# Storing each output tile as two halves from two queues, SyncE and GpSimd, in a mixture-of-experts dispatch kernel

## The chip, the cores and the metric

The kernel runs on one core of one Trainium2 chip. The metric is the device time of one execution in microseconds: before the change the median of three runs is 240.65 us (240.26 to 240.80). The profiled execution took 240.13 us, of which the trace covers a span of 238.3 us, from the first instruction to the last.

## The reference

Every token's row of 512 fp32 values is written out twice (k = 2), each copy multiplied by one of the token's two expert weights. The expert indices are an input, but they don't enter the result.

```python
batch, seq, hidden, n_experts = 16, 1024, 512, 8      # k = 2

def reference(x, expert_indices, expert_weights):
    x_expanded = x[:, :, np.newaxis, :].repeat(k, axis=2)
    weights = expert_weights[..., np.newaxis]
    return (x_expanded * weights).astype(np.float32)
```

The input x is 16384 rows of 2 KB, 33.55 MB; the output is twice that, 67.11 MB; the weights are 0.13 MB. There is one multiplication for each output element and nothing else.

## The kernel before

The 16384 tokens are cut into eight tiles of 2048 tokens. Partition p of a tile holds 16 consecutive tokens, so that what one partition loads is 32 KB contiguous in x and what it stores is 64 KB contiguous in the output. The list `groups` (line 35) and the function `rows` (line 48) say this.

Three pools hold the buffers. `w_tile` has all weights, 256 for each partition, loaded at the start by eight small transfers on SyncE's queue (line 57). `x_tile` has two buffers of 32 KB per partition. `o_tile` has two buffers; one is shaped `[P, 2, HALF * row + PAD]` (line 88), two halves of eight tokens each, 32 KB per partition and half. The padding of eight elements keeps the two halves apart in the buffer.

`load(i)` (lines 71 to 79) loads a whole x tile, 4 MB (4096 KB in the profile), with one transfer on ScalarE's queue (line 78). Tiles 0 and 1 are loaded ahead. The main loop (line 83) then does, for tile i and each of its 16 tokens t, two multiplications of 128 x 512 elements by a weight for each partition: the first copy on VectorE (`tensor_scalar`, line 99), the second on ScalarE (`mul`, line 93). Both write to half `h = t // HALF` of `o_tile`.

The stores are all on SyncE's queue (line 109). Tile 0 is stored as two halves of 4 MB, the first as soon as its eight tokens are done. Each of the tiles 1 to 7 is stored with one transfer of 8 MB (8192 KB in the profile) after the last token, and the two halves of a partition are two runs of 32 KB in it. So nine stores are issued. After its multiplications, tile i asks for the load of tile i + 2 (the call stands right behind the store).

The semaphores, and the order of the instructions on each engine, are set by the tile framework and aren't written out in the kernel. Two rules of it matter here. The first multiplication of tile i + 2 waits until the whole of `o_tile` of tile i has been stored, both halves, since the buffer is given back as one. And the framework may place the issue of a load somewhat later in ScalarE's stream than the loop has it: the load of tile 3 goes out at 53.37 us, behind the first multiplication of tile 2.

Of the kernel before, what the change touches and what calls it, by code (L numbers as in the profile page):

```python
# [1 line left out]

# [4 lines left out]


@with_exitstack
def kernel(  # L10
    ctx: ExitStack,
    tc: tile.TileContext,
    x: bass.AP,
    expert_indices: bass.AP,
    expert_weights: bass.AP,
    out: bass.AP,
):
    nc = tc.nc

    batch, seq, hidden = x.shape  # L20
    k = expert_weights.shape[-1]
    P = nc.NUM_PARTITIONS
    ntok = batch * seq
    assert ntok % P == 0
    A_TOTAL = ntok // P

    f32 = mybir.dt.float32
    row = k * hidden
    TX = 16
    TO = 16  # L30
    HALF = TO // 2
    PAD = 8


    groups = [[16], [16], [16], [16], [16], [16], [16], [16]]
    assert sum(sum(g) for g in groups) == A_TOTAL

    xf = x.rearrange("b s h -> (b s) h")
    of = out.rearrange("b s k h -> (b s) (k h)")
    wf = expert_weights.rearrange("b s k -> (b s) k")  # L40

    w_pool = ctx.enter_context(tc.tile_pool(name="w_pool", bufs=1))
    x_pool = ctx.enter_context(tc.tile_pool(name="x_pool", bufs=2))
    o_pool = ctx.enter_context(tc.tile_pool(name="o_pool", bufs=2))

    w_tile = w_pool.tile([P, A_TOTAL * k], f32)

    def rows(of_all, done, T):
        return of_all[done * P : (done + T) * P, :].rearrange(
            "(p a) n -> p (a n)", a=T  # L50
        )

    weights = []
    for group in groups:
        weights.append((sum(n for _, n in weights), sum(group)))
    for at, T in weights:
        nc.sync.dma_start(out=w_tile[:, at * k : (at + T) * k], in_=rows(wf, at, T))  # L57

    tiles = []
    done = 0  # L60
    for group in groups:
        T = sum(group)
        a0 = 0
        for n in group:
            tiles.append((done, T, a0, n))
            a0 += n
        done += T

    loaded = []

    def load(i):
        if i >= len(tiles):
            return
        done, T, a0, n = tiles[i]
        x_tile = x_pool.tile([P, TX * hidden], f32)
        cols = rows(xf, done, T)[:, a0 * hidden : (a0 + n) * hidden]
        for lo, hi in [(0, P)]:
            nc.scalar.dma_start(out=x_tile[lo:hi, : n * hidden], in_=cols[lo:hi, :])
        loaded.append(x_tile)

    for i in range(2):
        load(i)
    for i, (done, T, a0, n) in enumerate(tiles):
        x_tile = loaded[i]
        outr = rows(of, done, T)
        for t in range(n):
            if t % TO == 0:
                o_tile = o_pool.tile([P, 2, HALF * row + PAD], f32)
            for kk in range(k):
                c = (done + a0 + t) * k + kk  # L90
                h, o = t // HALF, t % HALF * row + kk * hidden
                if kk == 1:
                    nc.scalar.mul(  # L93
                        out=o_tile[:, h, o : o + hidden],
                        in_=x_tile[:, t * hidden : (t + 1) * hidden],
                        mul=w_tile[:, c : c + 1],
                    )
                    continue
                nc.vector.tensor_scalar(  # L99
                    out=o_tile[:, h, o : o + hidden],  # L100
                    in0=x_tile[:, t * hidden : (t + 1) * hidden],
                    scalar1=w_tile[:, c : c + 1],
                    scalar2=None,
                    op0=mybir.AluOpType.mult,
                )

            if t + 1 == TO or (i == 0 and t + 1 == HALF):
                halves = slice(h if i == 0 else 0, h + 1)
                nc.sync.dma_start(  # L109
                    out=outr.rearrange("p (b n) -> p b n", b=2)[:, halves, :],  # L110
                    in_=o_tile[:, halves, : HALF * row],
                )
        load(i + 2)

# [1 line left out]
_INS = ['x', 'expert_indices', 'expert_weights']  # L116
_OUTS = [((16, 1024, 2, 512), 'float32')]


# [23 lines left out]
```

## Time and profile before

| What | Value |
|---|---|
| time, median of three | 240.65 us |
| span of the trace | 238.3 us |
| moved by DMA | 100.81 MB (33.69 MB read from HBM, 67.11 MB written) |
| mean DMA rate over the span | 423 GB/s |
| VectorE busy | 51.4 us (22%), 128 instructions of 481 ns |
| ScalarE busy | 80.6 us (34%), 128 instructions of 708 ns |
| GpSimd busy | 0.2 us, four memsets at the start |
| whole-tile stores, issue to landing | 47.8 us median (7 of them) |
| half stores of tile 0, issue to landing | 25.4 us median |
| loads, issue to landing | 23.3 us median (8 of them) |

The profile numbers the hardware queues: q1 carries what SyncE issues (weights and stores), q10 what ScalarE issues (the loads). Shares of a queue are shares of the time of the core's 16 DMA engines. A packet is one run moved by one engine; nearly all bytes here move in packets of 32 KB. In a view by windows or slices a packet counts where it starts, so in short slices a share can be above 1 and in its neighbour below.

### The profile page before, as it was taken

To read this page: it belongs to the slowest core of one execution; us is meant where nothing else is said; L and a number is where in the kernel's file an instruction comes from. 1 tells how busy PE (TensorE), PEld (TensorE's weight loads), DVE (VectorE), ACT (ScalarE), POOL (GpSimd) and SP (SyncE) were. 2 spreads that over 40 slices of the span, in tenths; PEclk is the share of its full clock that TensorE was granted. 3 is DMA by queue.
4 is the path that set the end of the run, shared out by engine and by line. 5 is a ranking of instruction groups with operands and counts; after the bars stand their busy time and mean duration, and the time that the engine had idled before them with its cause. 6 is when DMAs were issued, how large, how long until landed. Compare 5 with 4: busy or idle time off the path is not lost.

```text
span 238.3 us, 364 instructions
## 1 busy us (share of the span) xinstructions
DVE 51.4 (22%) x128; ACT 80.6 (34%) x129; POOL 0.2 (0%) x4
## 2 busy tenths in 40 slices
DVE  0082900009000027000055003700008206400000
ACT  0288960009600039300059003930008706900000
POOL 0000000000000000000000000000000000000000
DMA  7999999999999999999999999999999999999996
GB/s 266 441 442 369 423 429 434 418 429 429 429 440 440 440 436 436 440 440 423 434 418 423 440 423 440 440 434 434 440 440 440 418 434 423 429 434 423 440 440 264
DMA packets 4498, 100.81 MB, mean 423 GB/s; under 512 B 1424, under 2 KB 1424, under 8 KB 1424
## 3 DMA queue, kind: packets, MB, share of 16 engines
q1 hardware_dynamic: 3344, 67.24, 65.6%
q10 hardware_dynamic: 1152, 33.55, 33.2%
q14 instruction: 2, 0.02, 0.0%
HBM read 33.69 MB, written 67.11 MB: 423 GB/s over the span
## 4 chain that ended last, share of the span: by engine, by line
DMA 70%; ACT 12%; another core or an unknown queue 4%; SPq 1%; issue 0%; ACTq 0%
DMA out_dram<-o_tile 51%; ACT o_tile L93 12%; DMA x_tile<-in_x_dram 10%; DMA w_tile<-in_expert_weights_dram 9%; SPq L57 1%; ACTq L138 0%; ACTq L93 0%; SPq L109 0%
## 5 line engine op out<-in xcount | busy, mean ns | idle before, releaser
L93 ACT ACTIVATE o_tile<-x_tile,w_tile 128x512 f32<-128x512 f32 x128 | 79.3, 708 | 119.7 <-DMA out_dram<-o_tile 115.7
L99 DVE TENSOR_SCALAR o_tile<-x_tile,w_tile 128x512 f32<-128x512 f32 x128 | 51.4, 481 | 153.9 <-DMA out_dram<-o_tile 136.6
L93 ACT ACT_TABLE_LOAD x1 | 1.3, 1283 | 8.5 <-DMA w_tile<-in_expert_weights_dram 8.5
L127 POOL MEMSET const-bfloat16-1.0<- 128x1 bf16 x1 | 0.1, 101 | 0.0
L127 POOL MEMSET const-uint8-127<- 128x1 uint8 x1 | 0.1, 101 | 0.0
L127 POOL MEMSET const-float32-0.0<- 128x1 f32 x1 | 0.1, 98 | 0.2 <-issue 0.2
L127 POOL MEMSET const-float32-1.0<- 128x1 f32 x1 | 0.1, 98 | 0.0
## 6 DMA issues: line engine op xcount, KB each, us to landing
out_dram<-o_tile SPq DMA_DIRECT2D x7, 8192.0 KB, 47.8
x_tile<-in_x_dram ACTq DMA_DIRECT2D x8, 4096.0 KB, 23.3
out_dram<-o_tile SPq DMA_DIRECT2D x2, 4096.0 KB, 25.4
w_tile<-in_expert_weights_dram SPq DMA_DIRECT2D x8, 16.0 KB, 21.0
```

What stands on the lines that cost most here:

```text
L57: nc.sync.dma_start(out=w_tile[:, at * k : (at + T) * k], in_=rows(wf, at, T))
L93: nc.scalar.mul(out=o_tile[:, h, o : o + hidden], in_=x_tile[:, t * hidden : (t + 1) * hidden], mul=w_tile[:, c : c + 1],)
L99: nc.vector.tensor_scalar(out=o_tile[:, h, o : o + hidden], in0=x_tile[:, t * hidden : (t + 1) * hidden], scalar1=w_tile[:, c : c + 1], sc ...
L127: nc = _bacc.Bacc("TRN2", target_bir_lowering=False, num_devices=1)
```

## The change

Two things are edited. The padding of `o_tile` goes, so that the two halves of a partition lie next to each other. And the store is cut in two for every tile, not only for tile 0: as soon as the eighth token is multiplied, the first half (4 MB) is stored by SyncE, and after the sixteenth token the second half (4 MB) is stored by GpSimd. So there are 16 stores of 4 MB, eight on each of the two engines, where there were nine, and GpSimd, which issued no transfer before, becomes a third queue beside SyncE's and ScalarE's. The loads stay on ScalarE's queue as they were. The purpose is to hand over the first half of a tile earlier, and to have two store queues that can be in flight side by side.

```diff
@@ -29,7 +29,6 @@
     TX = 16
     TO = 16
     HALF = TO // 2
-    PAD = 8
@@ -85,7 +84,7 @@
         for t in range(n):
             if t % TO == 0:
-                o_tile = o_pool.tile([P, 2, HALF * row + PAD], f32)
+                o_tile = o_pool.tile([P, 2, HALF * row], f32)
@@ -104,11 +103,11 @@
-            if t + 1 == TO or (i == 0 and t + 1 == HALF):
-                halves = slice(h if i == 0 else 0, h + 1)
-                nc.sync.dma_start(
-                    out=outr.rearrange("p (b n) -> p b n", b=2)[:, halves, :],
-                    in_=o_tile[:, halves, : HALF * row],
+            if (t + 1) % HALF == 0:
+                store = nc.sync if h == 0 else nc.gpsimd
+                store.dma_start(
+                    out=outr[:, h * HALF * row : (h + 1) * HALF * row],
+                    in_=o_tile[:, h, : HALF * row],
                 )
```

## The prediction

> **What bounds the kernel now.** I read the strip of 40 slices first, because it says whether any resource is full all the way.
>
> ```profile
> DVE  0082900009000027000055003700008206400000
> ACT  0288960009600039300059003930008706900000
> DMA  7999999999999999999999999999999999999996
> ```
>
> Both computing engines are idle most of the time; the 16 DMA engines are full in every slice but the first and the last. The chain of waits agrees: 70% of it is DMA, 51% the stores. The issues say that the stores aren't limited by their issue, since one takes 47.8 us to land and two are in flight.
>
> The next question is at what rate a full DMA engine runs, and whether two queues change it. The DMA view of two windows answers, the first with stores (q1) and loads (q10) together, 100 to 117 us, the second with stores alone, 210 to 230 us:
>
> ```profile
> DMA packets 224, 7.34 MB, mean 432 GB/s; under 512 B 0, under 2 KB 0, under 8 KB 0
> q1 hardware_dynamic: 112, 3.67, 49.9%
> q10 hardware_dynamic: 112, 3.67, 49.9%
> ```
>
> ```profile
> DMA packets 279, 8.62 MB, mean 431 GB/s; under 512 B 16, under 2 KB 16, under 8 KB 16
> q1 hardware_dynamic: 279, 8.62, 99.7%
> ```
>
> Mixed: 0.499 x 16 engines x 17 us = 135.7 us over 112 packets of 32 KB is 1.212 us for one. Stores alone: 0.997 x 16 x 20 us = 319 us over 263 packets (279 less 16 small ones [...]) is 1.213 us. So a packet takes the same time whether one queue or two feed the engine, two queues share it packet by packet, and there is no gap: shares add up to 99.7 and 99.8%. In the middle, from 60 to 230 us, the same view gives 433 GB/s.
>
> All 100.81 MB at 433 GB/s would be 232.8 us, and the span is 238.3. The other 5.5 us lie at the ends. Nothing moves before about 1.7 us. From 2 to 24 us the mean is 400 GB/s, which costs 22 x (1 - 400/433) = 1.7 us. At the other end (window 234 to 238.3 us) the last packets start near 236.0 us, so the last lands near 237.2, and 1.1 us of closing instructions follow. The sum is 1.7 + 1.7 + 1.1 = 4.5; about 1 us is left for small gaps and for DMA engines that end before the last one. This is all that a rearrangement of the same bytes could win.
>
> Last, the chain in order of time around the first stores:
>
> ```profile
> 2.11 21.93 DMA w_tile<-in_expert_weights_dram
> 24.04 0.02 issue
> 24.05 0.03 SPq L109
> 24.08 0.03 issue
> 24.11 29.06 DMA out_dram<-o_tile
> 53.17 0.02 issue
> 53.19 0.04 ACTq L93
> ```
>
> SyncE issued the second half of tile 0 at 24.05 us, held by a weight transfer, although ScalarE had finished tile 0 at 13.03 + 9.91 = 22.94. And tile 2 starts when that store lands at 53.17: the buffer is given back only with its second half.
>
> [...] The trace of before has no transfer from GpSimd, so neither its packets nor its cost is shown. [...]
>
> **The change, part by part.**
>
> Bytes and packets: 16 stores of 4 MB in place of two of 4 MB and seven of 8 MB. Packets stay 32 KB if GpSimd's are cut as SyncE's. Tile 0 is stored by halves already, so the half's form is in the trace: from 25 to 45 us q1 moves 128 such packets in 48.6% of 16 x 20 us, 1.215 us each. Cutting costs 7 stores x 16 more small packets, 112 packets; the 16 in the middle of the window above leave no visible trace. Cost 0.
>
> Padding: only the distance between halves in the buffer. Instructions keep their shape. Cost 0.
>
> Earlier first half: SyncE issues it after 8 of 16 multiplications, 5 us sooner (half of 9.91). The DMA engines are full with the previous tile's store then, hence 0. For the last tile, too: it starts at 198.87 us when tile 5's store has landed, and tile 6's 8.39 MB are still to come, 19.4 us at 433 GB/s, while computing takes 9.91 us. The same margin rules out a hole anywhere. When tile i starts computing, the store of tile i - 1 is queued, on both queues now; even if one were drained and only the other's 4.19 MB were left, these last 9.7 us at full rate, and the next first half arrives after 5 us.
>
> Loads: with two store queues and one load queue in turn a load gets a third of 433 GB/s, not half: 4.19 MB in 29.1 us in place of 19.4. A tile's load and stores are 12.58 MB, 29.1 us at full rate, so load and stores then come in together. A load that comes late leaves more of the engines to the stores. Cost 0.
>
> Waits: GpSimd's store waits for the sixteenth multiplications of both engines. Behind it in its queue are only later second halves, and for them waits the tile two further on, which waited for the whole tile before as well. The weight wait of 24.04 - 22.94 = 1.1 us goes for the second half of tile 0, but SyncE's first half was queued by then (18.07 us): window 22 to 24 us shows a DMA share of 0.93, so at most 0.14 us is won. [...] Cost 0.
>
> [...] A third of the bytes, 8 stores, comes from GpSimd. [...]
>
> Sum: 240.65 + 0.68 - 0.0 = 241.3 us.
>
> **Rivals.** No change: [...] all other parts cost 0. For it speak the packets of unchanged length with one and two queues; against it, only that GpSimd's path isn't in the trace. It gives 240.65 us. Faster: the DMA engines that share the last packets better end together. In the window 234 to 238.3 us engines start 47.8% of 4.3 us = 2.06 us of packets each; with some 0.6 us of a packet begun before 234, they stop on average near 236.7, the last near 237.2. Two queues could level these 0.5 us, and 0.14 us come from the start: 240.0 us. [...] Far slower, inside my first case: GpSimd's packets being smaller than 32 KB, or one slow DMA engine[...].
>
> **How the numbers follow.** Forecast, slower by descriptor work: 0.45, at 241.3 us. No change: 0.33, at 240.65. Faster: 0.22, at 240.0. [...] the runs before spread by 0.54 us. To leave out one in ten on each side I take 239.8 to 243.5. Faster, same and slower by 0.2% (0.48 us) are the three cases: 0.22, 0.33, 0.45.
>
> **What would show it.** A third queue with 1024 packets of 32 KB and 128 small ones, and about 33% of the DMA time; packets of q1 and q10 still at 1.213 us. For the forecast: packets of the new queue longer than that, or shares that add up to less than 99.7% in mid-kernel windows. For no change: the 433 GB/s stand. Computing starts some 29 us apart. It would be wrong altogether if the new queue's packets are of another size, if a hole appears in the strip, or if the start or the close grows with GpSimd's part in it.

## The result and the profile after

The changed kernel takes 253.24 us (median of four, 250.87 to 254.38), the kernel before 240.50 us beside it. The ratio is 1.0516, 95% interval 1.0434 to 1.0598: slower by about 5%, where 0.3% was forecast, and above the whole range of 239.8 to 243.5 us. The profiled execution took 250.87 us, the lowest of the four, with a span of 249.1 us for 238.3.

The strip of 40 slices of the kernel after, tenths of busy time:

```profile
DVE  0082900000900001900008200090001900045000
ACT  0287950000950001950008700096001940049100
DMA  7999999999999999999999999999999999996995
```

The DMA engines are as full as before, but for one slice near the end. Yet the same 100.81 MB took 10.8 us more. The queues of the page (packets, MB, share of the 16 engines' span), before and after, say where:

```profile
q1 hardware_dynamic: 3344, 67.24, 65.6%
q10 hardware_dynamic: 1152, 33.55, 33.2%
```

```profile
q10 hardware_dynamic: 1152, 33.55, 33.4%
q1 hardware_dynamic: 2304, 33.69, 32.8%
q0 software_dynamic: 1152, 33.55, 31.3%
```

Added up the shares are 97.5% of 249.1 us, so a DMA engine was busy 242.9 us; before it was 98.8% of 238.3, 235.4 us. It was not busy for 6.2 us, before for 2.9. (The shares are rounded, so these sums are good to some 0.4 us.) So the loss has two parts: **7.5 us more packet time** for the same packets, and **3.3 us more of not moving anything**. This account, shares times span and the rest, is used for every experiment below.

*Packet time.* The DMA view of the stretch 40 to 100 us, kernel after:

```profile
DMA packets 849, 24.54 MB, mean 409 GB/s; under 512 B 100, under 2 KB 100, under 8 KB 100
q1 hardware_dynamic: 304, 8.78, 38.8%
q0 software_dynamic: 314, 9.24, 36.0%
q10 hardware_dynamic: 231, 6.52, 25.6%
```

Share x 16 x 60 us over the number of 32 KB packets in the bytes gives 1.39 us a packet for SyncE's stores (q1, 268 packets), 1.226 us for GpSimd's (q0, 282), 1.235 us for the loads (q10, 199). From 100 to 220 us the same working gives 1.214, 1.213 and 1.327 us: then the loads are the long ones. Before, all were at 1.21 us. In this kernel GpSimd's own packets hardly lengthen; those of the others do.

These are means, and they hide two kinds of packets. Read packet by packet from the trace, 178 of SyncE's 268 packets took at most 1.25 us, as before, and 73 took more than 1.4 us: 1.83 us on average, 2.46 at most. Of the 512 loads from 100 to 220 us, 371 are as before and 103 above 1.4 us. Before the change 2241 of 2244 packets from 60 to 230 us took at most 1.25 us. So in these stretches a fifth to a good quarter of the packets of one queue take up to about twice as long, and the others take about what they took. "Long packets" below means this: a higher mean by such a part of them.

*Not moving.* Windows of the kernel after (VectorE, ScalarE and GpSimd busy, clock, DMA share, GB/s):

```profile
221.00:223.00 2.00, 1.76 (x5) 1.78 (x3) 0.00 (x0) 1.00 0.99 426
223.00:225.00 2.00, 2.00 (x6) 2.00 (x5) 0.00 (x0) 1.00 0.46 197
225.00:227.00 2.00, 2.00 (x6) 2.00 (x5) 0.00 (x0) 1.00 0.12 49
227.00:229.00 2.00, 0.66 (x2) 2.00 (x4) 0.00 (x0) 1.00 1.19 508
```

From 223 to 227 us the engines miss 2 x (0.54 + 0.88) = 2.8 us, while the last tile is being computed. The waits of VectorE (us in total, times, longest) before and after, and the chain of waits in order of time, tell why it is computed so late:

```profile
DVE o_tile L99 <- DMA out_dram<-o_tile: 136.6, 6, 28.0
```

```profile
DVE o_tile L98 <- DMA x_tile<-in_x_dram: 145.5, 7, 30.6
```

```profile
192.29 28.82 DMA x_tile<-in_x_dram
221.11 0.03 issue
221.14 0.05 DVEq L98
221.19 0.05 issue
221.24 2.07 DVE o_tile L98 x5
```

Before, a store ended the wait of each of the tiles 2 to 7; now a load does for the tiles 3 to 7, and loads are 69% of the chain. Such a load takes 29 to 37 us, and only then the next tile starts. By 221 us the stores of the tile before are nearly through. Earlier tiles have no such hole (DMA share 0.93 to 1.04 in the six microseconds from 98, 130, 160 and 190 us), because the next load goes out as they start; behind the last tile there is none.

The loads also go out later than before, though their lines weren't edited. The timeline of ScalarE around the load of tile 7, before and after:

```profile
146.87 9.91 ACT L93 ACTIVATE o_tile<-x_tile,w_tile 128x512 f32<-128x512 f32 x16 [15.30 <-DMA out_dram<-o_tile]
156.80 0.33 ACTq L78 DMA_DIRECT2D x_tile<-in_x_dram  x1
```

```profile
162.81 9.28 ACT L92 ACTIVATE o_tile<-x_tile,w_tile 128x512 f32<-128x512 f32 x15
...
192.21 0.72 ACT L92 ACTIVATE o_tile<-x_tile,w_tile 128x512 f32<-128x512 f32 x1 [20.12 <-DMA x_tile<-in_x_dram]
192.29 0.33 ACTq L77 DMA_DIRECT2D x_tile<-in_x_dram  x1
```

Before, it was issued as soon as tile 5 was multiplied (156.8 us), and so were the loads of tiles 4, 5 and 6 behind tiles 2, 3 and 4. Now tile 5 is multiplied at 172.1 us, but the load stands behind ScalarE's first multiplication of tile 6 and goes out 20 us later. The order on an engine is the framework's; why it placed the loads differently isn't shown. In e1 below, which differs only in having no store from GpSimd, they go out as before.

### The profile page after: what moved, and what is told of

Its sections match the earlier page's. It is cut to its first block, busy times and chain, and to the rows that moved or that the text cites. A ratio compares the mean times of both kernels' runs of the same rounds, so it can differ in the third digit from the quotient of the medians.

```text
span 249.1 us, 382 instructions
## 1 busy us (share of the span) xinstructions
DVE 51.4 (21%) x128; ACT 80.7 (32%) x129; POOL 4.6 (2%) x12
## 2 busy tenths in 40 slices
DMA packets 4610, 100.81 MB, mean 405 GB/s; under 512 B 1536, under 2 KB 1536, under 8 KB 1536
## 4 chain that ended last, share of the span: by engine, by line
DMA 84%; ACT 4%; DVE 2%; issue 2%; POOLq 0%; DVEq 0%; ACTq 0%
DMA x_tile<-in_x_dram 69%; DMA out_dram<-o_tile 15%; ACT o_tile L92 4%; DVE o_tile L98 2%; POOLq L137 0%; DVEq L137 0%; ACTq L92 0%; DVEq L98 0%; POOLq L108 0%
## 5 line engine op out<-in xcount | busy, mean ns | idle before, releaser
L108 POOL DMA_DIRECT2D out_dram<-o_tile x8 | 4.4, 548 | 227.1 <-ACT o_tile L92 227.1
## 6 DMA issues: line engine op xcount, KB each, us to landing
x_tile<-in_x_dram ACTq DMA_DIRECT2D x8, 4096.0 KB, 29.9
out_dram<-o_tile SPq DMA_DIRECT2D x8, 4096.0 KB, 29.9
```

What stands on the lines that cost most here:

```text
L108: store.dma_start(out=outr[:, h * HALF * row : (h + 1) * HALF * row], in_=o_tile[:, h, : HALF * row],)
```

## The experiments

Names stand for theories: H, stores in halves; S, GpSimd's queue by itself; T, three queues at once; R, three queues at once, one of them with GpSimd's stores; M and P, two store streams (for P one of them from GpSimd) beside loads; D, DMA engines out of step; L, late loads and their hole. Others are explained in the expectations that use them. The account of all runs, in us; each ratio is to executions of the kernel before made beside the run (medians 240.38 to 241.68 us):

| Kernel | time, median | ratio to before (95%) | span | busy | not busy |
|---|---|---|---|---|---|
| before | 240.65 | 1 | 238.3 | 235.4 | 2.9 |
| after | 253.24 | 1.043 to 1.060 | 249.1 | 242.9 | 6.2 |
| e1_halves_sync | 240.11 | 0.9951 to 0.9984 | 238.4 | 235.3 | 3.1 |
| e2_whole_gpsimd | 242.39 | 1.0024 to 1.0076 | 241.1 | 236.5 | 4.6 |
| e3_loads_gpsimd | 243.24 | 1.007 to 1.013 | 243.4 | 237.3 | 6.1 |
| e4_loads_sync | 255.64 | 1.057 to 1.066 | 252.5 | 244.2 | 8.3 |
| e6_whole_alternate | 253.73 | 1.046 to 1.057 | 251.9 | 240.6 | 11.3 |
| e7_weights_scalar | 256.07 | 1.058 to 1.068 | 253.9 | 244.8 | 9.1 |
| e8_loads_two_queues | 250.27 | 1.035 to 1.044 | 248.1 | 237.2 | 10.9 |
| e9_shifted_engines | 244.11 | 1.009 to 1.017 | 242.2 | 236.6 | 5.6 |
| e10_gpsimd_four_tiles | 250.43 | 1.037 to 1.048 | 247.8 | 244.3 | 3.5 |
| e11_few_loads (less work) | 182.63 | 0.758 to 0.761 | 180.8 | 177.0 | 3.8 |
| e12_gpsimd_loads_too | 250.21 | 1.036 to 1.048 | 249.2 | 240.7 | 8.5 |
| e13_scalar_halves | 258.49 | 1.073 to 1.078 | 256.7 | 242.3 | 14.4 |
| e14_spread_engines | 249.71 | 1.017 to 1.046 | 247.9 | 239.0 | 8.9 |
| e15_sbuf_loads | 272.50 | 1.109 to 1.142 | 270.4 | 264.2 | 6.2 |
| e16_sbuf_loads_sync | 249.83 | 1.017 to 1.047 | 248.4 | 241.4 | 7.0 |

### The change without GpSimd (e1), and GpSimd without the change (e2)

```diff
-                store = nc.sync if h == 0 else nc.gpsimd
+                store = nc.sync
```

> All 16 half stores from SyncE, no padding; the only difference from the changed kernel is that GpSimd's queue is gone. Theory S [...] and theory T (three queues in flight lengthen packets): 240.6 us within 0.5, packets of 32 KB at 1.213 us. Theory H (stores in half form, whose runs of 32 KB lie 64 KB apart in the output, lengthen packets): 246 us or more, with a mean packet of q1 or q10 above 1.25 us. Theory L (part of the loss is a hole near 221 us, since the loads, at a third of the rate, come in last): no hole here, as loads get half the rate again.

It takes 240.11 us, ratio 0.9968: 0.3% under before. The stretch 40 to 200 us:

```profile
DMA packets 2389, 69.32 MB, mean 433 GB/s; under 512 B 272, under 2 KB 272, under 8 KB 272
q1 hardware_dynamic: 1619, 47.28, 68.5%
q10 hardware_dynamic: 768, 22.02, 31.9%
```

0.685 x 16 x 160 over 1443 packets and 0.319 x 16 x 160 over 672 are both 1.215 us. H falls: cutting every tile into halves, handing the first over early and dropping the padding cost nothing. There is no hole either (3.1 us not busy). The whole loss comes with the queue of the second half.

The second run puts all stores of the kernel before on GpSimd's queue (whole tiles, padding kept):

```diff
-                nc.sync.dma_start(
+                nc.gpsimd.dma_start(
```

> The kernel before with all its stores issued by GpSimd in place of SyncE: nine stores, whole tiles with padding, and only two queues with large packets. Theory S: 246 us or more, with load packets above 1.25 us[...]. Theory T and theory H: 240.6 us within 1, packets at 1.213 us on both queues.

It takes 242.39 us, 0.5% more than before, with 1.1 us more busy time, though two thirds of all bytes now come from GpSimd's queue, twice as many as in the change. From 60 to 230 us:

```profile
DMA packets 2407, 73.06 MB, mean 430 GB/s; under 512 B 176, under 2 KB 176, under 8 KB 176
```

S as an explanation by itself falls. A small cost stays, which T and H didn't have: the time is 0.8 us above their range.

### Other roles for three queues (e4, e7, e6, e3, e8)

e4 issues loads from SyncE, first halves from ScalarE, second halves from GpSimd; e7 is the same with the weights on ScalarE's queue.

```diff
-            nc.scalar.dma_start(out=x_tile[lo:hi, : n * hidden], in_=cols[lo:hi, :])
+            nc.sync.dma_start(out=x_tile[lo:hi, : n * hidden], in_=cols[lo:hi, :])
...
-                store = nc.sync if h == 0 else nc.gpsimd
+                store = nc.scalar if h == 0 else nc.gpsimd
```

> The changed kernel with loads issued by SyncE and first halves by ScalarE; second halves by GpSimd still. A load is now issued as soon as its buffer is free and doesn't stand behind ScalarE's first multiplication of the next tile. Theory L: the hole of some 3 us goes, the tiles are gated by stores and not by loads, time 3 us under the changed kernel's, near 250 us. Theories S, T and H: long packets stay, 7 to 8 us more packet time for each DMA engine than before. If the issue order is the whole cause: 240.6 us.

> As e4_loads_sync (loads SyncE, first halves ScalarE, second halves GpSimd), with the weights on ScalarE's queue, so that the first load isn't issued behind eight weight transfers. Theory T plus L: neither late start nor hole are left, only long packets, so the time is that of before plus the excess: 240.5 + 7 to 9 = 248 to 249.5 us. If the late loads were the cause of the long packets too: near 241 us.

The hole goes in e4, as L expected: the share is 1.00 in the windows 215 to 225 and 225 to 245 us, and stores gate the tiles. Long packets stay: 244.2 us busy, 8.8 more than before. So late loads aren't what makes packets long. Here it is GpSimd's own packets that are the longest, other than in the change (40 to 210 us; q1 has the loads, q10 the first halves):

```profile
q0 software_dynamic: 803, 23.63, 35.5%
q1 hardware_dynamic: 801, 23.49, 32.5%
q10 hardware_dynamic: 800, 23.07, 32.5%
```

They take 0.355 x 16 x 170 / 721 = 1.34 us, the others 1.23 and 1.26. Which queue's packets lengthen depends on the roles.

The time of e4 was not 250 us, though, but 255.64: the first load is issued at 4.47 us for 0.73, behind eight weight transfers. e7 was to remove that and come out at 248 to 249.5 us. It missed, with 256.07 us. Its windows:

```profile
234.00:242.00 8.00, 0.00 (x0) 0.00 (x0) 0.00 (x0) 1.00 1.01 434
242.00:247.00 5.00, 0.00 (x0) 0.00 (x0) 0.00 (x0) 1.00 0.67 288
247.00:254.00 7.00, 0.00 (x0) 0.00 (x0) 0.00 (x0) 1.00 0.21 89
```

The stores were all issued long before, but the DMA engines finish far apart: from 242 us on, 5 x 0.33 + 7 x 0.79 = 7.2 us are not used. What a single engine lost isn't shown.

e6 stores whole tiles (with padding) in turn from SyncE and GpSimd, e3 lets GpSimd load and stores the halves from SyncE and ScalarE, e8 has all stores on GpSimd and each load cut in two, by columns, on SyncE and ScalarE.

```diff
# e6, on the kernel before
-                nc.sync.dma_start(
+                store = nc.sync if i % 2 == 0 else nc.gpsimd
+                store.dma_start(
# e3, on the kernel after
-            nc.scalar.dma_start(out=x_tile[lo:hi, : n * hidden], in_=cols[lo:hi, :])
+            nc.gpsimd.dma_start(out=x_tile[lo:hi, : n * hidden], in_=cols[lo:hi, :])
...
-                store = nc.sync if h == 0 else nc.gpsimd
+                store = nc.sync if h == 0 else nc.scalar
# e8, on e2
-        for lo, hi in [(0, P)]:
-            nc.scalar.dma_start(out=x_tile[lo:hi, : n * hidden], in_=cols[lo:hi, :])
+        half = n * hidden // 2
+        for q, c in [(nc.sync, 0), (nc.scalar, half)]:
+            q.dma_start(out=x_tile[:, c : c + half], in_=cols[:, c : c + half])
```

> The kernel before with whole tiles stored in turn by SyncE (even tiles) and GpSimd (odd tiles): three queues with large packets, whole-tile form. Theory T and theory S: load and SyncE packets lengthened, above 1.25 us on average, 246 us or more. Theory H: packets at 1.213 us, time near 240.6 but for a possible hole, since two tiles share the rate and come in together.

> Three queues with exchanged roles: loads from GpSimd, first halves from SyncE, second halves from ScalarE. Theory T (three queues with large packets at once lengthen them[...]): excess packet time (over 1.213 us a packet) of 6 to 9 us for each DMA engine, as in the changed kernel. Theory S2 (stores from GpSimd beside stores from another queue are the cause): excess near the 1.5 us of before, time 240 to 243 us unless a hole opens.

> Each load cut into two halves of 2 MB by columns, one from SyncE and one from ScalarE (16 KB packets in place of 32 KB), all stores whole from GpSimd: three queues, but two load streams and one store stream. Theory T: lengthened packets while loads are in flight, time 244 us or more. Theory M (two store streams beside a load are needed): packets of the stores at 1.213 us and of the loads at half of it, time within 1 us of e2_whole_gpsimd, about 242 us.

e6: long packets (5.2 us more busy; from 100 to 130 us SyncE's take 1.39 us), although tiles are stored whole, and a large hole besides (DMA share 0.29 from 200 to 210 us), as two tiles in flight come in together: VectorE starts tile 6 at 200.10 us and tile 7 at 207.42, each when a store has landed.

e3: only 1.9 us more busy time than before, far from T's 6 to 9. Three queues are not enough to lengthen packets, in the profiled execution. Its windows show a hole nearly alone, and its chain what the last tile waited for:

```profile
205.00:211.00 6.00, 0.00 (x0) 0.00 (x0) 0.00 (x0) 1.00 0.70 300
211.00:214.00 3.00, 2.07 (x6) 2.09 (x4) 0.00 (x0) 1.00 0.48 208
```

```profile
185.16 26.64 DMA out_dram<-o_tile
```

6 x 0.30 + 3 x 0.52 = 3.4 us are missed around the start of the last tile, about as much as in the change, but for another reason. Tile 7 waits for a store: the second half of tile 5, which ScalarE issues only behind its first multiplication of tile 6 (185.16 us), though tile 5 was multiplied at 167.2. One caution: e3's fourteen executions spread from 241.8 to 256.2 us, three of them at 249 or more, which the ratio leaves out, and the profiled one took 245.2; what the long ones did was not seen.

e8 takes 250.27 us, which would fit T, but not for T's reason. From 60 to 230 us it runs at 434 GB/s: two load streams beside GpSimd's stores don't lengthen anything. Most of the loss is at the start, where the DMA share is 0.45 from 20 to 30 us. The timeline there:

```profile
20.52 9.59 DVE L100 TENSOR_SCALAR o_tile<-x_tile,w_tile 128x512 f32<-128x512 f32 x24 [9.14 <-DMA x_tile<-in_x_dram]
25.84 4.40 POOL L110 DMA_DIRECT2D out_dram<-o_tile  x1 [25.39 <-ACT o_tile L94]
30.75 0.53 POOL L110 DMA_DIRECT2D out_dram<-o_tile  x1 [0.51 <-ACT o_tile L94]
```

Two delays add up. SyncE issues its half of the first load only at 8.49 us, behind eight weight transfers, so that ScalarE multiplies tile 0 from 20.52 us on and its first half is stored from 25.84 (before: 13.03 and 18.07). And GpSimd's issue of this store lasts 4.40 us in place of 0.53. It ends at 30.24 us, just after VectorE's row of multiplications (30.11 us). Whether VectorE held it up isn't shown by this one issue in one execution. In the changed kernel GpSimd's issues are 0.55 us on average, and VectorE is idle during all eight (its row of tile 1 ends at 31.18 us, the issue behind it comes at 34.99).

### The streams one by one (e10, e11, e12, e13)

```diff
# e10
-                store = nc.sync if h == 0 else nc.gpsimd
+                store = nc.gpsimd if h == 1 and i < 4 else nc.sync
# e11: loads of tiles 2 to 7 left out
-        x_tile = loaded[i]
+        x_tile = loaded[i % 2]
...
-        load(i + 2)
# e12
-            nc.scalar.dma_start(out=x_tile[lo:hi, : n * hidden], in_=cols[lo:hi, :])
+            nc.gpsimd.dma_start(out=x_tile[lo:hi, : n * hidden], in_=cols[lo:hi, :])
# e13
-                store = nc.sync if h == 0 else nc.gpsimd
+                store = nc.sync if h == 0 else nc.scalar
```

> Stores as in the changed kernel (SyncE first halves, GpSimd second halves), but only the first two x tiles are loaded and used in turn for all eight: the loads of tiles 2 to 7 are left out, so the work is 75.6 MB in place of 100.8. Theory P: with two store streams and no load packets stay at 1.213 us, so the span is about 75.6 MB at 433 GB/s, 174.6 us, and the 5.5 us of the ends: 180 us, and a time near 182.5. If the two store streams alone lengthen packets as in the changed kernel (8 us in 29 us x 6 of three streams): 186 us or more.

Measured 182.63 us, 182.5 expected. From 30 to 170 us:

```profile
q0 software_dynamic: 1040, 30.41, 50.3%
q1 hardware_dynamic: 1031, 30.11, 49.8%
```

0.503 x 16 x 140 over 928 packets is 1.214 us, and 0.498 x 16 x 140 over 919 the same. SyncE's and GpSimd's stores side by side are harmless as long as nothing is loaded.

> First halves from SyncE; second halves and loads both from GpSimd, in one queue: two queues with large packets, but a GpSimd store stream still runs beside a SyncE store stream and loads. Theory P (the mix of streams, not the number of queues): packets lengthen, excess 4 us or more over before. Theory R [...]: packets at 1.213 us; the time then is 240.5 us plus what holes cost, since a load stands behind a store in the queue.

R falls, and P's 4 us or more come true. There are two queues with large packets, and 5.3 us more busy time than before; from 70 to 220 us SyncE's packets take 0.339 x 16 x 150 / 640 = 1.271 us. The number of queues is not the cause.

> The changed kernel, but only the second halves of tiles 0 to 3 go to GpSimd; those of tiles 4 to 7 to SyncE, as in e1_halves_sync. Theory P (a store stream from GpSimd, one from SyncE and a load stream in flight together lengthen packets): excess packet time falls to about half, 3 to 5 us over before while GpSimd's stores run, and near 0 once they have landed; no hole near the end, as loads get half the rate again: 244 to 246 us. If the loss is a fixed cost of using GpSimd's queue at all: near 250 us.

The timing in the kernel is as P said, the size is not. While GpSimd's stores run (30 to 150 us) and after (160 to 240 us):

```profile
DMA packets 1647, 48.15 MB, mean 401 GB/s; under 512 B 176, under 2 KB 176, under 8 KB 176
...
DMA packets 1183, 34.57 MB, mean 432 GB/s; under 512 B 128, under 2 KB 128, under 8 KB 128
```

The rate drops to 401 GB/s and recovers fully. 120 x (1 - 401/433) = 8.9 us are lost on four stores, not half of 7.5 us. The change itself lost 60 x (1 - 409/433) = 3.3 us from 40 to 100 us and 120 x (1 - 419/433) = 3.9 us from 100 to 220. The loss isn't proportional to GpSimd's bytes. The time, 250.43 us, is where the expectation had a fixed cost of using GpSimd's queue; but the loss is spread over GpSimd's stores and ends with them, which a fixed cost wouldn't do. And one more thing can be read here. The loads go out late as in the change (tile 7's at 181.6 us, tile 5 multiplied at 167.2), but at the end only two queues share the rate, and there is no hole: the DMA share is 1.00 to 1.01 from 200 to 218 us. In e4 loads go out early beside three queues, and there is none either. As far as these two runs show, the hole of the change takes both, late loads and a third of the rate.

> The same arrangement without GpSimd: first halves from SyncE, second halves and loads both from ScalarE. Two store streams and a load stream[...]. Theories P and R: packets at 1.213 us, 240.5 us plus holes. If two store streams beside loads are enough whoever issues them: lengthened as in the changed kernel.

Neither reading fits. Packets don't stay at 1.213 us: there is 6.9 us more busy time without GpSimd, near the 7.5 of the change. But the form is another: five short bursts, each after a hole. The holes (14.4 us not busy) come mainly from the order on ScalarE, which issues a tile's second half and the load behind it only after its first multiplication of the next tile (63.09 and 63.48 us, behind 62.99). One burst and what follows, 74 to 79 and 79 to 92 us:

```profile
q1 hardware_dynamic: 32, 1.05, 68.5%
q10 hardware_dynamic: 28, 0.39, 23.0%
...
q10 hardware_dynamic: 92, 3.01, 53.7%
q1 hardware_dynamic: 80, 2.62, 46.7%
```

SyncE's 32 packets in the first stretch take 0.685 x 16 x 5 / 32 = 1.71 us, in the second 0.467 x 16 x 13 / 80 = 1.214. So P isn't the whole rule: GpSimd's stores are not needed for a burst, but of these kernels the lasting form with loads from HBM is seen only where a store stream from GpSimd runs beside another store stream and loads (after, e4, e6, e7, e10, e12). A pair of store streams without GpSimd that runs beside loads all the time was tried only in e3, whose loads came from GpSimd.

### Engines out of step, and loads from SBUF (e9, e14, e15, e16)

```diff
# e9, on e1: two small loads at the start
+    shift = w_pool.tile([8, 3072], f32)
+    nc.sync.dma_start(out=shift[:, :2048], in_=xf[0:32, :].rearrange("(p a) n -> p (a n)", a=4))
+    nc.sync.dma_start(out=shift[0:4, 2048:], in_=xf[0:8, :].rearrange("(p a) n -> p (a n)", a=2))
# e14, on e1: four small loads at the start
+    for c in (8, 4, 2, 1):
+        nc.sync.dma_start(
+            out=shift[0:c, :],
+            in_=xf[0 : 6 * c, :].rearrange("(p a) n -> p (a n)", a=6),
+        )
# e15, on the kernel after; e16, on e1
-            nc.scalar.dma_start(out=x_tile[lo:hi, : n * hidden], in_=cols[lo:hi, :])
+            src = cols[lo:hi, :] if i < 2 else loaded[i - 1][lo:hi, : n * hidden]
+            nc.scalar.dma_start(out=x_tile[lo:hi, : n * hidden], in_=src)
```

> e1_halves_sync (two queues only) with two additional small loads at the start [...]. Theory D (long packets come from DMA engines that are out of step with each other): packets lengthen all the way, 243 us or more. Theories T and M: packets stay at 1.213 us, time 240.1 us plus at most 0.5.

> As e9_shifted_engines, two queues only, but with four loads of 12 KB rows at the start [...]. Theory D2 (what lengthens packets is that the DMA engines are a packet or more apart in the same transfer): packets above 1.25 us in the middle of the kernel, 246 us or more. Theory P: packets at 1.213 us after the start, 241 to 246 us by the longer start alone.

The loads have rows of 8 and 4 KB in e9 and of 12 KB in e14. Each row was meant to set the DMA engine that moves it back by its time: from 1.213 us for 32 KB the author's estimate is 0.30 to 0.45 us in e9 and 0.45 to 1.8 us in e14. No view names the engine of a packet, so that the engines fell behind each other isn't shown. Both kernels are slower (244.11 and 249.71 us), but not in the middle: e9 runs at 432 GB/s from 30 to 190 us, and e14 at 432 GB/s from 50 to 190, and there the packets of the two queues take 1.214 and 1.213 us in e9, 1.216 and 1.222 in e14. So these loads don't lengthen packets later, and nothing speaks for D in the form tried. (Both times lie above the expected ones, mostly by the longer start, with a DMA share of 0.87 from 10 to 20 us in e9 and of 0.75 from 20 to 30 us in e14, before 1.07 and 1.00; in e14 the engines also end further apart, with a DMA share of 0.51 from 240 us on.)

> The changed kernel with the loads of tiles 2 to 7 taken from the other x buffer in SBUF in place of HBM (so its output is that of other tokens; HBM is read for two tiles only). Streams, queues and bytes are as in the changed kernel. Theory HBM (the lengthening is reads and writes of HBM getting into each other's way): packets at 1.213 us, excess near that of before. Theory SBUF (it is inside the DMA engines or at SBUF's side): still 5 us or more excess.

> The same for the two-queue kernel e1_halves_sync: loads of tiles 2 to 7 from SBUF (the output is that of other tokens). The control for e15_sbuf_loads: it shows what a packet from SBUF to SBUF takes without GpSimd's stores. Theories HBM and SBUF both: packets near 1.213 us, about 240 us, unless such a packet takes longer by itself.

e15 takes 272.5 us: its load packets, now from SBUF to SBUF, take 0.411 x 16 x 174 / 640 = 1.79 us from 66 to 240 us, its store packets 1.23 to 1.24. The control e16 was to show that such packets aren't long by themselves, at about 240 us. It takes 249.83 us and shows something else. Its stretches 50 to 125 and 132 to 190 us:

```profile
q1 hardware_dynamic: 687, 19.89, 61.5%
q10 hardware_dynamic: 419, 12.58, 38.9%
...
q1 hardware_dynamic: 485, 14.16, 57.1%
q10 hardware_dynamic: 277, 8.36, 43.2%
```

In the first the packets of q10 take 0.389 x 16 x 75 / 384 = 1.216 us, in the second 0.432 x 16 x 58 / 255 = 1.57 us. Same two queues, same transfers: the packets of tiles 2 to 5 are short, and of those of tiles 6 and 7, 70 and 85 of 128 are long (about 1.8 us), from the first to the last of the transfer, while the others still take 1.21. So long packets need no reads of HBM while they last, and whether they appear can switch within one execution. Whether they have the same origin as in the change isn't shown.

## Why the prediction was wrong

- **Halves, padding, earlier first half: right.** e1 puts their sum at 0 or a little below (240.11 us); the profile doesn't show where its 0.3% comes from, its span being that of before.
- **Packet size and GpSimd's waits: right.** GpSimd's queue has the 1024 packets of 32 KB and 128 small ones that were forecast, and its issues take 0.53 to 0.67 us.
- **The 0.68 us of the sum: too much.** It was the author's estimate of what descriptor work for GpSimd's transfers adds on the DMA engines; neither that work nor its cost is shown by a run, and the upper end of the range rested on it too. GpSimd's packets take 0.313 x 16 x 249.1 / 1024 = 1.218 us in place of 1.213, which is 64 x 0.005 = 0.3 us for an engine on average; the reason isn't shown. This term alone set the direction of the forecast, and it isn't what made the kernel slower: that the direction came true is luck.
- **The step that failed first** is the one from the two-queue window: "a packet takes the same time whether one queue or two feed the engine". It was shown for stores and loads from SyncE and ScalarE (1.212 and 1.213 us), and the sum used it for a third stream from GpSimd, with 0.68 us added. The term that was missing is the lengthening of the *other* queues' packets, nearly all of the 7.5 us in the profiled execution.
- **The second** is the term "Loads" at cost 0, with "The same margin rules out a hole anywhere". That a load gets a third of the rate was right (29.9 us median for 23.3). But the prediction kept the loads' place: in the change they go out 20 to 27 us after the tile that used their buffer is multiplied, behind the first multiplication of the next tile, and then gate it. "A load that comes late leaves more of the engines to the stores" is right until the stores have nothing left (DMA share 0.46 and 0.12 from 223 to 227 us). That is 2.8 of the 3.3 us more of not moving. e4 (early loads) and e10 (half the rate at the end) have no hole.
- The prediction named both signs, q1 and q10 not at 1.213 us and a hole in the strip, but gave them no size in the sum.
- **What stays open** is why packets lengthen. It needs no halves (e6), no third queue (e12), no late loads (e4), and no reads of HBM (e16, with the reserve made there). Halves (e1), all stores from GpSimd's queue (e2), three queues (e3, e8), two store streams without loads (e11) and small loads at the start (e9, e14) are each not enough. In e10 it ends when GpSimd's stores end (401 GB/s, then 432). What happens at a single DMA engine isn't shown, since no view here names the engine of a packet.

## What to carry to other kernels

With the DMA engines full, another queue brought no rate here (432 GB/s with two store queues in e11, 433 before), and in the change it took some (409 and 419 GB/s): measure the packet time with the very mix of streams that the change makes, not with the mix of before. Split the span into shares times span and the rest, for one then sees at once whether packets got longer or engines stood still. And when a stream is added, ask which transfer gets a smaller part of the rate, when that transfer is issued, and who starts only when it has landed. Look too at the order on each engine after the change: a load whose line wasn't edited went out 20 us later. Here the version to keep is the halves from SyncE alone (e1, 240.11 us, 0.3% under before).

## What the runs showed of the hardware that was not expected

- Packets of 32 KB have a median of 1.213 us in the changed kernel too. The mean of SyncE's stores rose to 1.39 us over 60 us because 73 of 268 packets took 1.83 us on average, when GpSimd's stores and loads ran beside them.
- GpSimd's own packets took 1.218 us in the changed kernel, but 1.34 us in e4, where SyncE loaded and ScalarE stored the first halves.
- Store queues of SyncE and GpSimd side by side moved 432 GB/s with no loads beside them (e11; 433 before). With loads beside them 3 to 7% of the rate was lost: 409 and 419 GB/s in the changed kernel, 401 in e10.
- In one execution of e16 the mean of a load's packets switched from 1.216 to 1.57 us between two loads of the same form.
- GpSimd's issue of a store lasted 4.40 us beside 24 multiplications of VectorE in a row (e8), and 0.53 and 0.67 us for the two issues behind it, without them.
